# Attention scores of a latent-attention layer: the two heads of a pair in row tiles of 64, and a head's three rotary products in one pass of 96 rows

## The chip, the core and the metric

The kernel runs on one core of a Trainium2 chip, as one program. The metric is the device time of one execution in microseconds (us), lower being better. A core has TensorE (PE in the profile; PEld is its loading of weights), VectorE (DVE), ScalarE (ACT), GpSimd (POOL) and SyncE (SP, whose queue issues the DMAs here). TensorE multiplies a stationary operand of up to 128 rows by 128 columns, the "weights", with a moving operand of the same rows and up to 512 columns. The rows are the dimension that is summed over. The result stands in a PSUM bank of 128 partitions by 512 fp32 values.

## What is computed

One inference step of a two-layer backbone for 1024 latent ("sample") and 256 context ("prompt") tokens, 1280 in all, with a model width of 1024. The first layer is windowed attention beside a matrix-memory recurrence. The second, in which the change lies, is multi-head latent attention:

```python
def _mixer_c(h, w_in, q_norm, w_qb, kv_norm, w_kvb, w_out, ctx, pos):
    qa, kva, kr, z = jnp.split(h @ w_in, C_SPLITS, axis=-1)
    q = (_rmsnorm(qa, q_norm) @ w_qb).reshape(B, T, C_HEADS, C_NOPE + C_ROPE)      # 16 heads, 64 + 32
    q_nope, q_rope = q[..., :C_NOPE], q[..., C_NOPE:]
    ...                                            # rotary positions on q_rope and kr of the sample tokens
    kv = (keys_ckv @ w_kvb).reshape(B, Tk, C_HEADS, C_NOPE + C_VDIM)
    k_nope, v = kv[..., :C_NOPE], kv[..., C_NOPE:]
    k = jnp.concatenate([k_nope, jnp.broadcast_to(keys_kr, (B, Tk, C_HEADS, C_ROPE))], axis=-1)
    qf = jnp.concatenate([q_nope, q_rope], axis=-1)[:, :, :, None, :]
    attn = _blocked_attn(qf, k, v, None, (C_NOPE + C_ROPE) ** -0.5)                # softmax(q k) v
    out = (attn * jax.nn.silu(z)) @ w_out
```

A head's query and key have 64 values of their own ("nope") and 32 rotary ones; the rotary key is the same for all heads. Sample tokens read 1280 keys (1024 of their own and 256 of a cache), prompt tokens the 256 of the prompt.

## The kernel before

Every fp32 operand of a product is split into a high part, rounded to the type fp32r, and the rest as a low part. A product then is three: high by high, high by low, low by high.

The second layer's attention is the class `Mla`. It goes through eight pairs of heads (`pair`, p = 0 to 7). Keys of a pair (`keys`, in three chunks of 512), queries (`queries`, in chunks of 512, 512 and 256 tokens) and values are made from the latents by products on TensorE, and split by `split_sb`: a cast to the high part on ACT, a subtraction for the low part on DVE. `fill` lists at which step of a pair the keys, queries and values of the next are made.

For the scores each head has tiles of its own for its query and its key (`cQ`, `cK`; high and low), in which the 64 nope rows and the 32 rotary rows stand below each other: 96 rows for the first head of a pair. For the second the nope rows come out of the product in partitions 64 to 127, so its tiles have 128 rows: 32 rows of zeros in the query, the 32 rotary ones, and then the 64. `spread` splits the two heads' halves of a product into their tiles, 64 partitions at a time, and DMAs bring the rotary rows from DRAM.

`scores(p)` is a generator over blocks of 256 query tokens and, within a block, the two heads one after the other. `part` issues the three products of one head, 128 queries by 512 keys (`one`) or by 256 (`both`, twice into one bank). A bank `S` goes to a maximum on DVE (`cmx`) and an exponential on ACT (`cPa`, `cPb`, `cPc`), and `finish` scales by the sums on POOL. `uses` then transposes the probabilities on TensorE into a bank `T` (line 107), splits them (`cph` on ACT, `cpl` on DVE), and multiplies with the values into a bank `V`. `pair` advances both: a step of `scores`, a step of `uses` once more than six steps are ahead, and what `fill` has due. All products pass through the helper of line 103, so the profile's rows are told apart by their tiles. `set_psum(S=3, T=3, V=1, mm=1)` shares out PSUM's eight banks.

The order in which the engines get their instructions isn't that of the code: the framework's scheduler (`schedule_with_timeline_sim=True`) reorders the instructions of each engine by a simulated timeline. [...]

Of the kernel before, what the change touches and what calls it, by code (L numbers as in the profile page):

```python
# [22 lines left out]
T = TS + TP  # L23
# [1799 lines left out]
def split_sb(K, src, h, l, scale=None):  # L1823

    nc = K.nc
    if scale is None:
        nc.scalar.copy(h, src)
        nc.vector.tensor_sub(l, src, h.bitcast(F32))
    else:
        nc.scalar.mul(h, src, scale)  # L1830
        nc.vector.scalar_tensor_tensor(l, src, scale, h.bitcast(F32), ALU.mult, ALU.subtract)


def layer_c(K):
    nc, I, d = K.nc, K.I, K.dc
# [17 lines left out]
    ps = K.psT()  # L1853
# [21 lines left out]
    C = Mla(K, wp, cq, ckv)  # L1875
# [9 lines left out]
    for ci, (t0, N) in enumerate(CHUNKS):  # L1885
        for k in (0, 1, 2, 3, 4):
# [22 lines left out]
    cu.release()  # L1909
    ap = C.ap = left("catt")  # L1910
    C.add_queries(ap)
    C.add_values(ap, sets[1])
    for c in range(3):
        C.keys(0, c)
# [2 lines left out]
        for i in range(2):  # L1917
            C.values(0, c, i)
    C.add_set(ap)
    K.set_psum(S=3, T=3, V=1, mm=1)  # L1920
    for p in range(7):
        C.pair(p, C.fill(p))

# [39 lines left out]
class Mla:  # L1963

    SLOTS = ((3, 4, 5), (0, 1, 2), (3, 5, 0), (4, 6, 1), (0, 2, 4), (3, 5, 1), (4, 6, 3), (0, 2, 1))

    def __init__(self, K, wp, cq, ckv):
        self.K, self.wp, self.cq, self.ckv = K, wp, cq, ckv  # L1970
        self.w, self.KV, self.Q, self.queue = {}, [], [], []
        self.wv = {}
        self.use, self.ahead, self.tail = self.uses(), 0, None

    def add_set(self, pool):
        K, kr, n = self.K, self.K.dc["kr"], len(self.KV)
        keys = [[pool.tile([128, 1536], F32R, tag=f"cK{n}{par}{s}", name=f"cK{n}{par}{s}") for s in range(2)]
                for par in range(2)]
        for s in range(2):
            K.dma(keys[0][s][64:96, :], kr[s])  # L1980
            for o in (0, 32):
                K.dma(keys[1][s][o:o + 32, :], kr[s])
        self.KV.append(keys)

    def add_values(self, *pools):

# [5 lines left out]
        self.V = {(p, c): tiles[i] for p, row in enumerate(self.SLOTS) for c, i in enumerate(row)}  # L1992

    def add_queries(self, pool):
        K = self.K
        for c, (_, N) in enumerate(CHUNKS):
            t = [[pool.tile([128, N], F32R, tag=f"cQ{c}{par}{s}", name=f"cQ{c}{par}{s}") for s in range(2)]
                 for par in range(2)]
            for s in range(2):
                K.nc.gpsimd.tensor_scalar(t[1][s][0:32, :], K.small.rearrange("p a f -> p (a f)")[0:32, 0:N], 0.0, 1.0, ALU.mult, ALU.mult)  # L2000
            self.Q.append(t)

    def weights(self, p):
        K, wp, nc = self.K, self.wp, self.K.nc
# [29 lines left out]
    def spread(self, ps, dst, cols):  # L2034

        for par in range(2):
            r = slice(par * 64, par * 64 + 64)
            split_sb(self.K, ps[r], *[t[r, cols] for t in dst[par]])

    def keys(self, p, c):  # L2040
        ps = self.K.ps()
        self.products(ps, self.w[p][1], [t[c] for t in self.ckv], 2)
        self.spread(ps, self.KV[p % 2], slice(c * 512, (c + 1) * 512))

    def values(self, q, c, i):

# [10 lines left out]
    def queries(self, p, ci):  # L2057
        K, (t0, N) = self.K, CHUNKS[ci]
        ps = K.ps()
        self.products(ps[:, 0:N], self.w[p][0], [t[ci] for t in self.cq], 3)  # L2060
        self.spread(ps[:, 0:N], self.Q[ci], slice(0, N))
        for par, r in ((0, 64), (1, 32)):
            h = (2 * p + par) % 4 * 32
            for s in range(2):
                K.dma(self.Q[ci][par][s][r:r + 32, :], K.dc["qr"][s][p // 2][h:h + 32, t0:t0 + N])

    def fill(self, p):

        q = (p + 1) // 2
        f = [(0, partial(self.queries, p, 1)), (2, partial(self.queries, p, 2)), (4, partial(self.weights, p + 1))]  # L2070
        if p % 2:
            f += [(8, partial(self.weights_v, q))]
            f += [(14 + 4 * i, partial(self.values, q, i // 2, i % 2)) for i in range(4)]
        elif p:
            f += [(7 + i, partial(self.values, q, 2, i)) for i in range(2)]
# [12 lines left out]

    def finish(self):
        while self.use_step():  # L2090
# [9 lines left out]

    def scores(self, p):

        K, nc, ap, keys = self.K, self.K.nc, self.ap, self.KV[p % 2]
        for t0, par in ((t0, par) for t0 in range(0, T, 256) for par in range(2)):
            sample = t0 < TS
            ci = t0 // 512
            rows = slice(0, 128 if par else 96)
            Q, KK = [t[rows] for t in self.Q[ci][par]], [t[rows] for t in keys[par]]
            P = {}
            mx = K.t(ap, [128, 2, 3], F32, "cmx", 3)  # L2110
            den = K.t(ap, [128, 2, 3], F32, "cden", 3)

            def part(bank, bo, b, k0, n):
                q0 = t0 - CHUNKS[ci][0] + b * 128
                qs = slice(q0, q0 + 128)
                o = bank[:, bo:bo + n]
# [3 lines left out]
                return o  # L2120

            def finish(b):
                st = K.t(ap, [128, 8], F32, "cst", 4)
                nm, wt, dw, rd = st[:, 0:1], st[:, 1:4], st[:, 4:7], st[:, 7:8]
                if sample:
                    nc.vector.tensor_reduce(nm, mx[:, b, :], AX.X, ALU.min)
                    nc.scalar.activation(wt, mx[:, b, :], AF.Exp, bias=nm, scale=-1.0)
                    nc.gpsimd.tensor_mul(dw, den[:, b, :], wt)
                    nc.vector.reduce_sum(rd, dw, axis=AX.X)
                    nc.vector.reciprocal(rd, rd)  # L2130
                    for c in range(3):
                        pv = P[b, c]
                        nc.gpsimd.tensor_scalar(pv, pv, wt[:, c:c + 1], rd, ALU.mult, ALU.mult)  # L2133
                else:
                    nc.vector.reciprocal(rd, den[:, b, 0:1])
                    nc.gpsimd.tensor_scalar(P[b, 0], P[b, 0], rd, 1.0, ALU.mult, ALU.mult)

            def both(k0, c):
                S = K.psS()
                t = K.t(ap, [128, 512], F32, "cPc", 4)  # L2140
                for b in range(2):
                    part(S, b * 256, b, k0, 256)
                nc.vector.tensor_reduce(mx[:, :, c], S.rearrange("p (b k) -> p b k", b=2), AX.X, ALU.max, negate=True)
                for b in range(2):
                    P[b, c] = t[:, b * 256:(b + 1) * 256]
                    nc.scalar.activation(P[b, c], S[:, b * 256:(b + 1) * 256], AF.Exp,
                                         bias=mx[:, b, c:c + 1], accum_out=den[:, b, c:c + 1])

            def one(b, c):
                S = K.psS()  # L2150
                part(S, 0, b, c * 512, 512)
                nc.vector.tensor_reduce(mx[:, b, c:c + 1], S, AX.X, ALU.max, negate=True)  # L2152
                P[b, c] = K.t(ap, [128, 512], F32, "cP" + "ab"[c], 4)
                nc.scalar.activation(P[b, c], S, AF.Exp, bias=mx[:, b, c:c + 1],  # L2154
                                     accum_out=den[:, b, c:c + 1])

            if sample:
                one(0, 0)
                yield
                one(0, 1)  # L2160
                yield
                both(1024, 2)
                finish(0)
                yield
                one(1, 0)
                yield
                one(1, 1)
                finish(1)
            else:
                both(1280, 0)  # L2170
                finish(0)
                finish(1)
            self.queue.append((p, par, t0, P))
            yield

    def uses(self):
# [75 lines left out]
```

## Time and profile before

| | |
|---|---|
| runs shown | 2643.43, 2643.76, 2644.60 us; median 2643.76 |
| the profiled execution | 2644.84 us, its span 2643.0 us |
| granted TensorE clock | 0.995 of full speed |
| busy, share of the span | PE 97%, PEld 86%, DVE 67%, ACT 53%, POOL 44% |
| the second layer's attention | from 1875 to about 2540 us |

The span is the time from the first to the last instruction. In the profile's rows a group is named by line, engine, operation and "out<-in" tiles with the sizes (rows*columns of the weights, then partitions x elements of the output or of the moving operand); behind "x" stands the count, then the busy time in us and the mean duration in ns, then the engine's idle time ahead of the group and what ended it. [...] In rows of single instructions the first number is the start in us and the second the duration; "x3" are three of a kind in a row.

### The profile page before, as it was taken

The page shows a single profiled execution, that of the slowest core. Times are in us where ns is not written, and L with a number is a line of the kernel's source. Part 1 is how long each engine was busy: PE and PEld are TensorE (multiplying, and loading weights), DVE is VectorE, ACT ScalarE, POOL GpSimd, SP SyncE. Part 2 cuts the span into 40 slices and gives each one's busy share as a digit, 9 for nine tenths or more (in the row PEclk, how much of TensorE's full clock was granted, in tenths as well). Part 3 has the DMA queues.
Part 4 walks back from the last instruction along what each step waited for, and adds up shares of the span by engine and source line. Part 5 has one row for each costly group of instructions (what it writes and reads, how often), then busy time and mean ns, then how long its engine had stood idle before and what let it go on. Part 6 is the DMA issues. An engine that isn't in the chain of part 4 may idle for free.

```text
span 2643.0 us, 48201 instructions
## 1 busy us (share of the span) xinstructions
PE 2572.9 (97%) x16209; PEld 2262.3 (86%) x16209; DVE 1777.3 (67%) x4040; ACT 1406.5 (53%) x3598; POOL 1167.1 (44%) x1533
## 2 busy tenths in 40 slices
PE   7989999999999999989999999999899999999998
PEld 6878899898998888868888877987799999999887
DVE  6883565655746666388777545335788888888853
ACT  5222443543533433287666533322788888888842
POOL 4342333423434434275545453223455545555642
PEclk9989999999999999999999999999999999999999
DMA  7554556556657655463433463333311101101333
GB/s 247 181 157 157 161 178 198 175 171 195 199 169 225 213 164 185 140 204 111 136 102 111 130 197 130 121 95 114 104 30 30 44 29 40 35 19 30 122 104 128
DMA packets 344586, 348.79 MB, mean 132 GB/s; under 512 B 29610, under 2 KB 291415, under 8 KB 344083
## 3 DMA queue, kind: packets, MB, share of 16 engines
q1 hardware_dynamic: 344338, 345.71, 42.1%
q8 instruction: 129, 2.11, 0.3%
q14 instruction: 119, 0.97, 0.1%
HBM read 235.09 MB, written 110.51 MB: 131 GB/s over the span
## 4 chain that ended last, share of the span: by engine, by line
PE 81%; DVE 6%; DMA 3%; ACT 3%; issue 3%; POOL 2%; SPq 1%; POOLq 0%; DVEq 0%; ACTq 0%
PE mm L103 34%; PE S L103 27%; PE V L103 8%; PE T L107 6%; PE D L103 3%; PE mm L107 2%; SPq L138 1%; PE T L103 1%; DVE macc L321 1%; DVE att_nm L1109 0%; DVE xT L536 0%; ACT att_p L1114 0%; POOL wl L354 0%; DMA o_x<-y 0%; DMA w<-in_w_out_ab 0%
## 5 line engine op out<-in xcount | busy, mean ns | idle before, releaser
L354 POOL TENSOR_TENSOR wl<-wf,wh 128x256 fp32r<-128x256 f32 (+2 forms) x288 | 250.7, 896 | 448.6 <-ACT wh L353 378.6
L103 PE MATMUL mm<-hTh,wh 128*128 128x512 f32 (+1 forms) x912 | 328.6, 360 | 1.6 <-DVE scr L620 0.9
L103 PE MATMUL mm<-hTl,wh 128*128 128x512 f32 (+1 forms) x912 | 325.5, 357 | 0.0
L103 PE MATMUL mm<-hTh,wl 128*128 128x512 f32 (+1 forms) x912 | 325.4, 357 | 0.0
L103 PE MATMUL S<-cK,cQ 96*128 96x512 f32 (+3 forms) x1248 | 298.3, 364 | 3.3 <-ACT cPb L2154 1.0
L2202 DVE TENSOR_TENSOR cpl<-T,cph 128x512 fp32r<-128x512 f32 x336 | 228.5, 685 | 38.0 <-ACT cph L2201 34.5
L103 PEld LDWEIGHTS S<-cK,cQ 96*128 96x128 f32 (+1 forms) x1248 | 192.8, 189 | 25.9 <-ACT cPb L2154 2.9
L2201 ACT CAST cph<-T 128x512 fp32r<-128x512 f32 x336 | 192.3, 589 | 26.6 <-PE T L107 13.4
L103 PEld LDWEIGHTS mm<-hTh,wl 128*128 128x128 f32 x912 | 172.0, 189 | 26.4
L103 PEld LDWEIGHTS mm<-hTh,wh 128*128 128x128 f32 x912 | 171.9, 188 | 25.7 <-DVE bmod L306 1.7
L103 PEld LDWEIGHTS mm<-hTl,wh 128*128 128x128 f32 x912 | 171.9, 188 | 22.9
L2152 DVE TENSOR_REDUCE cmx<-S 128x1 f32<-128x512 f32 x256 | 172.7, 681 | 16.4 <-PE S L103 15.2
L103 PE MATMUL V<-cph,cV 128*128 128x256 f32 x672 | 177.0, 290 | 1.0 <-DVE co L2217 1.0
L103 PE MATMUL V<-cpl,cV 128*128 128x256 f32 x672 | 171.9, 285 | 1.3 <-DVE cpl L2202 1.3
L103 PE MATMUL S<-w,o_ah 128*128 128x512 f32 x492 | 152.1, 395 | 3.0 <-ACT w L819 1.9
L103 PE MATMUL mm<-w,o_ah 128*128 128x512 f32 x468 | 151.4, 402 | 0.0
L2133 POOL TENSOR_SCALAR cPa<-cPa,cst 128x512 f32<-128x512 f32 x128 | 99.3, 776 | 118.0 <-DVE cst L2130 87.5
L1123 POOL TENSOR_SCALAR att_p<-att_p,att_den 128x640 f32<-128x640 f32 (+1 forms) x128 | 97.5, 774 | 103.4 <-DVE att_den L1120 41.0
L1134 ACT CAST att_ph<-mm 128x512 fp32r<-128x512 f32 x168 | 98.5, 586 | 81.5 <-PE mm L107 80.0
L353 ACT CAST wh<-wf 128x256 fp32r<-128x256 f32 (+2 forms) x288 | 102.0, 409 | 70.1 <-DMA wf<-in_w_in_ab 30.5
L1135 DVE TENSOR_TENSOR att_pl<-mm,att_ph 128x512 fp32r<-128x512 f32 x168 | 115.7, 689 | 32.1 <-ACT att_ph L1134 27.3
L103 PE MATMUL mm<-wh,hTh 128*128 128x256 f32 x480 | 135.8, 283 | 0.0
(432 smaller groups left out, 7823.5 us busy)
## 6 DMA issues: line engine op xcount, KB each, us to landing
wf<-in_w_in_ab SPq DMA_DIRECT2D x120, 256.0 KB
in<-in SPq DMA_DIRECT2D x40, 514.0 KB
in<-in SPq DMA_DIRECT2D x32, 386.0 KB
mw<-in_w_mod SPq DMA_DIRECT2D x48, 256.0 KB
in<-scr SPq DMA_DIRECT2D x40, 258.0 KB
o_x<-y SPq DMA_DIRECT2D x20, 512.0 KB
wm<-in_w_mod SPq DMA_DIRECT2D x16, 512.0 KB
in<-cx SPq DMA_DIRECT2D x32, 256.0 KB
```

The costliest lines, as they stand in the source:

```text
L103: return self.nc.tensor.matmul(out, lhsT, rhs, start=start, stop=stop)
L107: self.nc.tensor.transpose(out, in_, self.ident[:p, :p])
L138: self.nc.sync.dma_start(f(out), f(in_))
L353: K.nc.scalar.copy(wh, wf[:, k])
L354: K.nc.gpsimd.tensor_sub(wl, wf[:, k], wh.bitcast(F32))
L1123: nc.gpsimd.tensor_scalar(pv, pv, den[:, i:i + 1], 1.0, ALU.mult, ALU.mult)
L1134: K.nc.scalar.copy(ph, self.T)
L1135: K.nc.vector.tensor_sub(pl, self.T, ph.bitcast(F32))
L2133: nc.gpsimd.tensor_scalar(pv, pv, wt[:, c:c + 1], rd, ALU.mult, ALU.mult)
L2152: nc.vector.tensor_reduce(mx[:, b, c:c + 1], S, AX.X, ALU.max, negate=True)
L2201: nc.scalar.copy(ph, T_)
L2202: nc.vector.tensor_sub(pl, T_, ph.bitcast(F32))
```

## The change

The nope rows and the rotary rows get products of their own.

- Nope: one tile of 128 rows holds both heads' 64 rows, for keys and for queries. `part` works on both heads at once, with a bank each, and alternates between them: the three products of the first head have rows 0 to 63, those of the second rows 64 to 127.
- Rotary: the three products of a head (high by high, high by low, low by high) are put below each other in 3 x 32 = 96 rows: `cQr` holds the query's high, high and low parts, `cKr` the key's high, low and high. One product of 96 rows adds all three to the bank. `cKr` is loaded once for all pairs.
- `spread` and the zero rows fall away: a product of keys or queries is split over 128 partitions at once. The loads of rotary query rows become six per chunk instead of four; those of the rotary keys three instead of twelve.
- `scores` yields once for both heads and `pair` counts two steps for it, starting `uses` at more than ten steps ahead. Statistics and probabilities have more buffers. PSUM has four banks `S` and two `T`, instead of three and three.

```diff
-    K.set_psum(S=3, T=3, V=1, mm=1)
+    K.set_psum(S=4, T=2, V=1, mm=1)
...
     def add_set(self, pool):
-        keys = [[pool.tile([128, 1536], F32R, tag=f"cK{n}{par}{s}", name=f"cK{n}{par}{s}") for s in range(2)]
-                for par in range(2)]
-        for s in range(2):
-            K.dma(keys[0][s][64:96, :], kr[s])
-            for o in (0, 32):
-                K.dma(keys[1][s][o:o + 32, :], kr[s])
-        self.KV.append(keys)
+        n = len(self.KV)
+        self.KV.append([pool.tile([128, 1536], F32R, tag=f"cK{n}{s}", name=f"cK{n}{s}") for s in range(2)])
+
+    def add_rotary(self, pool):
+        K = self.K
+        self.kr = pool.tile([96, 1536], F32R, tag="cKr", name="cKr")
+        for i, s in enumerate((0, 1, 0)):
+            K.dma(self.kr[i * 32:i * 32 + 32, :], K.dc["kr"][s])
...
     def keys(self, p, c):
-        self.spread(ps, self.KV[p % 2], slice(c * 512, (c + 1) * 512))
+        split_sb(self.K, ps, *[t[:, c * 512:(c + 1) * 512] for t in self.KV[p % 2]])
...
     def queries(self, p, ci):
-        self.spread(ps[:, 0:N], self.Q[ci], slice(0, N))
-        for par, r in ((0, 64), (1, 32)):
+        split_sb(K, ps[:, 0:N], *self.Q[ci])
+        for par in range(2):
             h = (2 * p + par) % 4 * 32
-            for s in range(2):
-                K.dma(self.Q[ci][par][s][r:r + 32, :], K.dc["qr"][s][p // 2][h:h + 32, t0:t0 + N])
+            for i, s in enumerate((0, 0, 1)):
+                K.dma(self.QR[ci][par][i * 32:i * 32 + 32, :], K.dc["qr"][s][p // 2][h:h + 32, t0:t0 + N])
...
-            self.ahead += 1
-            if self.ahead > 6 and self.use_step():
-                next(self.use)
-            while fill and fill[0][0] <= n:
-                fill.pop(0)[1]()
-            n += 1
+            self.ahead += 2
+            for _ in range(2):
+                if self.ahead > 10 and self.use_step():
+                    next(self.use)
+                while fill and fill[0][0] <= n:
+                    fill.pop(0)[1]()
+                n += 1
...
-        for t0, par in ((t0, par) for t0 in range(0, T, 256) for par in range(2)):
+        for t0 in range(0, T, 256):
...
-                K.mm(o, Q[0][:, qs], KK[0][:, k0:k0 + n], True, False)
-                K.mm(o, Q[0][:, qs], KK[1][:, k0:k0 + n], False, False)
-                K.mm(o, Q[1][:, qs], KK[0][:, k0:k0 + n], False, True)
+                for i, (q, k) in enumerate(((qh, kh), (qh, kl), (ql, kh))):
+                    for par in range(2):
+                        r = slice(par * 64, par * 64 + 64)
+                        K.mm(banks[par][:, bo:bo + n], q[r, qs], k[r, ks], i == 0, False)
+                for par in range(2):
+                    K.mm(banks[par][:, bo:bo + n], QR[par][:, qs], self.kr[:, ks], False, True)
```

What becomes of the order on TensorE, as the two programs are built. The first place is the start of the third block of sample tokens (queries 512 to 767) of the first pair. Before, TensorE's queue holds this for the first head, where each number behind `S` is a bank of scores (128 queries by 512 keys):

```order
L103 MATMUL S_23370<-cK_22274,cQ_22673 128x512
L103 MATMUL S_23370<-cK_22275,cQ_22673 128x512
L103 MATMUL S_23370<-cK_22274,cQ_22674 128x512
L103 MATMUL V_23116<-cph_23217,cV_22689 128x256
L103 MATMUL S_23390<-cK_22274,cQ_22673 128x512
L103 MATMUL S_23390<-cK_22275,cQ_22673 128x512
L103 MATMUL S_23390<-cK_22274,cQ_22674 128x512
```

In the changed program TensorE's queue has this for the same block; `S_23308` and `S_23358` are banks of the first head, in rows 0 to 63, `S_23309` is one of the second, in rows 64 to 127, and `cKr,cQr` is the product of 96 rows:

```order
L103 MATMUL S_23308<-cK_22274,cQ_22663 128x512
L103 MATMUL S_23308<-cK_22275,cQ_22663 128x512
L103 MATMUL S_23308<-cK_22274,cQ_22664 128x512
L103 MATMUL S_23308<-cKr,cQr_22665 128x512
L103 MATMUL S_23309<-cK_22274,cQ_22663 128x512
L103 MATMUL S_23309<-cK_22275,cQ_22663 128x512
L103 MATMUL S_23309<-cK_22274,cQ_22664 128x512
L103 MATMUL S_23309<-cKr,cQr_22666 128x512
L103 MATMUL S_23358<-cK_22274,cQ_22663 128x512
L103 MATMUL S_23358<-cK_22275,cQ_22663 128x512
L103 MATMUL S_23358<-cK_22274,cQ_22664 128x512
L103 MATMUL S_23358<-cKr,cQr_22665 128x512
```

The code issues the products of the two banks in turns; the scheduler has moved them apart, so that one head's three and its rotary product come before the other head's.

The second place is TensorE's queue in the same block, for queries 640 to 767. Before, the first head's products of that bank stand between products for the next queries (`mm`) and transposes:

```order
L103 MATMUL mm_24004<-cq_22254,wql_22969 128x512
L103 MATMUL S_23446<-cK_22274,cQ_22673 128x512
L103 MATMUL S_23446<-cK_22275,cQ_22673 128x512
L103 MATMUL S_23446<-cK_22274,cQ_22674 128x512
L107 MATMUL T_23355<-small,cPb_23114 128x128
```

In the changed program the two heads' banks for these queries stand in TensorE's queue like this:

```order
L103 MATMUL S_23482<-cK_22274,cQ_22663 128x512
L103 MATMUL S_23483<-cK_22274,cQ_22663 128x512
L103 MATMUL S_23482<-cK_22275,cQ_22663 128x512
L103 MATMUL S_23483<-cK_22275,cQ_22663 128x512
L103 MATMUL S_23482<-cK_22274,cQ_22664 128x512
L103 MATMUL S_23483<-cK_22274,cQ_22664 128x512
L103 MATMUL S_23482<-cKr,cQr_22665 128x512
L103 MATMUL S_23483<-cKr,cQr_22666 128x512
```

Here the turns are kept; of 128 places with products of 512 columns, three are left in this way.

More of the change, by code (lines that the diff above doesn't have):

```diff
@@ L1911, in layer_c @@
     C.add_queries(ap)
+    C.add_rotary(ap)
     C.add_values(ap, sets[1])
@@ L1970, in __init__ @@
         self.K, self.wp, self.cq, self.ckv = K, wp, cq, ckv
-        self.w, self.KV, self.Q, self.queue = {}, [], [], []
+        self.w, self.KV, self.Q, self.QR, self.queue = {}, [], [], [], []
         self.wv = {}
@@ L1994, in add_queries @@
     def add_queries(self, pool):
-        K = self.K
         for c, (_, N) in enumerate(CHUNKS):
-            t = [[pool.tile([128, N], F32R, tag=f"cQ{c}{par}{s}", name=f"cQ{c}{par}{s}") for s in range(2)]
-                 for par in range(2)]
-            for s in range(2):
-                K.nc.gpsimd.tensor_scalar(t[1][s][0:32, :], K.small.rearrange("p a f -> p (a f)")[0:32, 0:N], 0.0, 1.0, ALU.mult, ALU.mult)
-            self.Q.append(t)
+            self.Q.append([pool.tile([128, N], F32R, tag=f"cQ{c}{s}", name=f"cQ{c}{s}") for s in range(2)])
+            self.QR.append([pool.tile([96, N], F32R, tag=f"cQr{c}{par}", name=f"cQr{c}{par}") for par in range(2)])
     def weights(self, p):
@@ L2032, in products @@
                 self.K.mm(out, st[a][:, k, :], mv[b][:, k, :], k + i == 0, k == kt - 1 and i == 2)
[L2034 to L2038, printed above, removed]
     def keys(self, p, c):
@@ L2074, in fill @@
         elif p:
-            f += [(7 + i, partial(self.values, q, 2, i)) for i in range(2)]
+            f += [(12 + i, partial(self.values, q, 2, i)) for i in range(2)]
         f += [(12 + 6 * c, partial(self.keys, p + 1, c)) for c in range(3)]
@@ L2101, in scores, with part, finish @@
     def scores(self, p):
-        K, nc, ap, keys = self.K, self.K.nc, self.ap, self.KV[p % 2]
-        for t0, par in ((t0, par) for t0 in range(0, T, 256) for par in range(2)):
+        K, nc, ap, (kh, kl) = self.K, self.K.nc, self.ap, self.KV[p % 2]
+        for t0 in range(0, T, 256):
             sample = t0 < TS
             ci = t0 // 512
[L2107 to L2113, printed above, removed]
-                q0 = t0 - CHUNKS[ci][0] + b * 128
-                qs = slice(q0, q0 + 128)
-                o = bank[:, bo:bo + n]
-                K.mm(o, Q[0][:, qs], KK[0][:, k0:k0 + n], True, False)
-                K.mm(o, Q[0][:, qs], KK[1][:, k0:k0 + n], False, False)
-                K.mm(o, Q[1][:, qs], KK[0][:, k0:k0 + n], False, True)
-                return o
-            def finish(b):
-                st = K.t(ap, [128, 8], F32, "cst", 4)
+            (qh, ql), QR = self.Q[ci], self.QR[ci]
+            P = [{}, {}]
+            mx = [K.t(ap, [128, 2, 3], F32, "cmx", 6) for _ in range(2)]
+            den = [K.t(ap, [128, 2, 3], F32, "cden", 6) for _ in range(2)]
+            def part(banks, bo, b, k0, n):
+                q0 = t0 - CHUNKS[ci][0] + b * 128
+                qs, ks = slice(q0, q0 + 128), slice(k0, k0 + n)
+                for i, (q, k) in enumerate(((qh, kh), (qh, kl), (ql, kh))):
[4 more added lines that the diff above has]
+                    K.mm(banks[par][:, bo:bo + n], QR[par][:, qs], self.kr[:, ks], False, True)
+            def finish(par, b):
+                st = K.t(ap, [128, 8], F32, "cst", 8)
@@ L2124, in finish @@
                 nm, wt, dw, rd = st[:, 0:1], st[:, 1:4], st[:, 4:7], st[:, 7:8]
                 if sample:
-                    nc.vector.tensor_reduce(nm, mx[:, b, :], AX.X, ALU.min)
-                    nc.scalar.activation(wt, mx[:, b, :], AF.Exp, bias=nm, scale=-1.0)
-                    nc.gpsimd.tensor_mul(dw, den[:, b, :], wt)
+                    nc.vector.tensor_reduce(nm, mx[par][:, b, :], AX.X, ALU.min)
+                    nc.scalar.activation(wt, mx[par][:, b, :], AF.Exp, bias=nm, scale=-1.0)
@@ L2129, in finish @@
+                    nc.gpsimd.tensor_mul(dw, den[par][:, b, :], wt)
                     nc.vector.reduce_sum(rd, dw, axis=AX.X)
@@ L2131, in finish @@
                     for c in range(3):
-                        pv = P[b, c]
+                        pv = P[par][b, c]
                         nc.gpsimd.tensor_scalar(pv, pv, wt[:, c:c + 1], rd, ALU.mult, ALU.mult)
                 else:
-                    nc.vector.reciprocal(rd, den[:, b, 0:1])
-                    nc.gpsimd.tensor_scalar(P[b, 0], P[b, 0], rd, 1.0, ALU.mult, ALU.mult)
+                    nc.vector.reciprocal(rd, den[par][:, b, 0:1])
+                    nc.gpsimd.tensor_scalar(P[par][b, 0], P[par][b, 0], rd, 1.0, ALU.mult, ALU.mult)
@@ L2138, in both @@
             def both(k0, c):
-                S = K.psS()
-                t = K.t(ap, [128, 512], F32, "cPc", 4)
+                banks = [K.psS() for _ in range(2)]
                 for b in range(2):
[L2142 to L2147, printed above, removed]
@@ L2149, in one @@
-            def one(b, c):
[L2150 to L2155, printed above, removed]
+                    part(banks, b * 256, b, k0, 256)
+                for par, S in enumerate(banks):
+                    t = K.t(ap, [128, 512], F32, "cPc", 4)
+                    nc.vector.tensor_reduce(mx[par][:, :, c], S.rearrange("p (b k) -> p b k", b=2), AX.X, ALU.max,
+                                            negate=True)
+                    for b in range(2):
+                        P[par][b, c] = t[:, b * 256:(b + 1) * 256]
+                        nc.scalar.activation(P[par][b, c], S[:, b * 256:(b + 1) * 256], AF.Exp,
+                                             bias=mx[par][:, b, c:c + 1], accum_out=den[par][:, b, c:c + 1])
@@ new lines, in one @@
+            def one(b, c):
+                banks = [K.psS() for _ in range(2)]
+                part(banks, 0, b, c * 512, 512)
+                for par, S in enumerate(banks):
+                    nc.vector.tensor_reduce(mx[par][:, b, c:c + 1], S, AX.X, ALU.max, negate=True)
+                    P[par][b, c] = K.t(ap, [128, 512], F32, "cP" + "ab"[c], 8)
+                    nc.scalar.activation(P[par][b, c], S, AF.Exp, bias=mx[par][:, b, c:c + 1],
+                                         accum_out=den[par][:, b, c:c + 1])
@@ L2162, in scores @@
                 both(1024, 2)
-                finish(0)
+                for par in range(2):
+                    finish(par, 0)
                 yield
@@ L2167, in scores @@
                 one(1, 1)
-                finish(1)
+                for par in range(2):
+                    finish(par, 1)
             else:
                 both(1280, 0)
-                finish(0)
-                finish(1)
-            self.queue.append((p, par, t0, P))
+                for par in range(2):
+                    for b in range(2):
+                        finish(par, b)
+            for par in range(2):
+                self.queue.append((p, par, t0, P[par]))
             yield
```

2 lines of the change are left out of this document (removed).

## Prediction

> **What bounds the kernel now.** I read the page's busy times and its chain first, then the busy times of the stage that the change touches (the attention of the second layer, 1875 to 2540 us), then its groups by shape, and last single TensorE instructions by start time.
>
> ```profile
> PE 2572.9 (97%) x16209; PEld 2262.3 (86%) x16209; DVE 1777.3 (67%) x4040; ACT 1406.5 (53%) x3598; POOL 1167.1 (44%) x1533
> PE 81%; DVE 6%; DMA 3%; ACT 3%; issue 3%; POOL 2%; SPq 1%; POOLq 0%; DVEq 0%; ACTq 0%
> core 0: us, PE busy (x) PEld busy (x) DVE busy (x) ACT busy (x) POOL busy (x), PEclk, DMA share, GB/s
> 1800.00:1875.00 75.00, 64.83 (x367) 54.39 (x365) 45.83 (x81) 29.34 (x62) 30.36 (x27) 0.95 0.47 146
> 1875.00:2540.00 665.00, 657.40 (x4512) 596.64 (x4513) 567.74 (x1300) 558.57 (x1531) 363.26 (x610) 1.00 0.14 44
> PE T L107 <- DVE cpl L2202: 1.8, 3, 0.8
> ```
>
> In the stage TensorE (PE) is busy for 657.4 of 665 us at full clock, and its longest wait in all is 1.8 us, on VectorE. DVE (568) and ACT (559) have some 100 us to spare. So a microsecond of PE work put in or taken out moves the end by about one; work saved on the other engines moves nothing. What a PE instruction costs is the distance between starts, since the printed durations overlap:
>
> ```profile
> 2142.69 0.86 PE L103 MATMUL S<-cK,cQ 128*128 128x512 f32 x3
> 2143.38 0.28 PE L103 MATMUL V<-cpl,cV 128*128 128x256 f32 x1
> 2143.73 0.60 PE L107 MATMUL T<-small,cPa 128*128 128x128 f32 x4
> 2150.80 0.88 PE L103 MATMUL S<-cK,cQ 96*128 96x256 f32 x6
> 2151.51 0.28 PE L103 MATMUL V<-cpl,cV 128*128 128x256 f32 x1
> L103 PE MATMUL S<-cK,cQ 96*128 96x512 f32 x384 | 114.3, 410 | 1.1 <-PE mm L103 1.0
> L103 PE MATMUL S<-cK,cQ 128*128 128x512 f32 x384 | 112.8, 407 | 1.1 <-ACT cPa L2154 0.6 <-ACT cPc L2146 0.5
> L103 PE MATMUL S<-cK,cQ 96*128 96x256 f32 x240 | 38.6, 293 | 0.0
> L103 PE MATMUL S<-cK,cQ 128*128 128x256 f32 x240 | 38.3, 291 | 1.1 <-ACT cPb L2154 1.0
> ```
>
> Three score products of 512 columns take 2142.69 to 2143.38, or 0.23 us each; six of 256 columns take 2150.80 to 2151.51, or 0.118 each. 96 rows cost what 128 cost. All score products: 768 x 0.232 + 480 x 0.1175 = 178 + 56 = 235 us.
>
> **The extra products.** Per head and bank there were three products; now there are three of 64 rows and one of 96. By themselves that is a third more: 256 x 0.232 + 160 x 0.1175 = 59 + 19 = **+78 us**. It is paid back only where a product in rows 0 to 63 runs at the same time as one in rows 64 to 127. If every one found its partner, half of 235 would go (117 us), and the net would be -39.
>
> **How many find it.** The scheduler does not keep the order in which the code writes them. Counted over the new PE order, of 1248 products of 64 rows only 21 (512 columns) and 18 (256) neighbours are in different row tiles; the usual run is three products of one head, its rotary product, then something else. Each product pairs once, which leaves about 12 and 11 pairs: 12 x 0.232 + 11 x 0.1175 = **-4 us**. No row of this trace shows two row tiles side by side; the bounds are 0 and -4.
>
> **The changes of row tile.** The new order enters the tile of 64 rows 424 times in this layer and leaves it 424 times, nearly always to the rotary product next. Before, it did so never there. What such a change costs shows where the first layer puts a transpose of few rows between wide products:
>
> ```profile
> 246.76 0.39 PE L103 MATMUL mm<-hTh,wl 128*128 128x512 f32 x1
> 246.99 0.40 PE L103 MATMUL mm<-hTh,wh 128*128 128x512 f32 x1
> 247.32 0.24 PE L107 MATMUL T<-small,modrow 32*128 32x32 f32 x1
> 247.49 0.50 PE L103 MATMUL mm<-hTl,wh 128*128 128x512 f32 x1
> 247.83 0.40 PE L103 MATMUL mm<-hTh,wl 128*128 128x512 f32 x1
> 247.31 0.13 PEld L107 LDWEIGHTS T<-small,modrow 32*128 32x128 f32 x1 [0.36 <-PE mm L103]
> 247.49 0.19 PEld L103 LDWEIGHTS mm<-hTl,wh 128*128 128x128 f32 x1
> 247.60 0.19 PEld L103 LDWEIGHTS mm<-hTh,wl 128*128 128x128 f32 x1
> 154.24 0.40 PE L103 MATMUL S<-hTh,wl 128*128 128x512 f32 x1
> 154.57 0.81 PE L107 MATMUL T<-small,rst 36*128 36x36 f32 x10
> 155.22 0.79 PE L107 MATMUL T<-small,gM 36*128 36x36 f32 x10
> 155.94 0.49 PE L103 MATMUL S<-hTh,wh 128*128 128x512 f32 x1
> 156.27 0.40 PE L103 MATMUL S<-hTl,wh 128*128 128x512 f32 x1
> ```
>
> Wide products start 0.23 apart (246.76, 246.99). Before the small one it is 0.33: 0.10 of standstill, and its weight load begins only at 247.31, where loads otherwise begin with the product before. Back again, the load starts with its own product (247.49) and the next start comes after 0.34: 0.11 of load that nothing covers, the 0.11 between the two loads. The rows at 154 to 156 (36 rows) give the same: 0.33 in, 0.33 out. The ten transposes there take 0.065 each, load and all; the one at 247.32 takes 0.17, so leaving costs 0.10 too. A change of tile thus costs 0.095 of standstill and 0.105 of bare load, 0.20 us, and in and out 0.40: 424 x 0.40 = 170 us. Of the entries 136 stand behind transposes, which start 0.11 apart ((0.60 - 0.27) / 3) though 128 columns stream in 0.23 / 4 = 0.058; some 0.05 of the standstill falls into that: -7. **+162 us.**
>
> The rows are of fp32 transposes; the new switches are between products, so the price is bounded by nothing from below and by the full 0.40 from above. I take 0.40, since both halves of the load and standstill appear at wide products of the same type, going in and coming out. [...]
>
> **What costs nothing.** Keys and queries are split once over 128 rows instead of twice over 64:
>
> ```profile
> L1827 ACT CAST cK<-mm 64x512 fp32r<-64x512 f32 x42 | 24.4, 580 | 3.6 <-DVE cK L1828 2.3 <-PE mm L103 0.7
> L1828 DVE TENSOR_TENSOR cK<-mm,cK 64x512 fp32r<-64x512 f32 x42 | 28.8, 685 | 2.9 <-ACT cK L1827 2.0
> L2201 ACT CAST cph<-T 128x512 fp32r<-128x512 f32 x330 | 188.9, 589 | 25.5 <-PE T L107 12.5 <-PE V L103 10.8
> L2202 DVE TENSOR_TENSOR cpl<-T,cph 128x512 fp32r<-128x512 f32 x330 | 224.4, 685 | 36.8 <-ACT cph L2201 33.5
> ```
>
> A cast takes 580 ns at 64 rows and 589 at 128, so half of them goes: 12 us of ACT and 14 of DVE on the keys, about as much on the queries. Both lie beside a full PE: 0. The rotary loads on SP's queue grow from 96 to 144, and the twelve of the keys become three; they are asked for at steps 0, 2 and 33 of a pair's 42 and read from steps 20, 40 and 42, at least nine steps of 665 / 8 / 42 = 2 us ahead, and no wait of PE on a DMA stands in the list whose first row is above: 0. Banks for transposed probabilities go from three to two. One is held for 0.44 + 0.59 + 0.69 = 1.7 us plus waits, so two pass one every 0.9 us, and 336 are needed in some 900 us, one per 2.7: 0. Without that cover, 0.1 us at each would be +34. Going the other way, PE's 7.6 us of idle time could be taken up.
>
> **Sum**, against the profiled execution's own 2644.84 us (span 2643.0): 2644.8 + 78 - 4 + 162 = 2881; less 1.1, since the median of the runs shown is 2643.76: **2880 us**. Its own range is 2840 to 2925: the idle time and price roundings (0.36 instead of 0.40 is -17) below, the T banks above.
>
> **Rivals.**
> - *Weights of the same tile are not loaded ahead* (12%). In runs of three, the second and third product would wait for a bare load: 1248 - 424 - 39 = 785 x 0.105 = +82: 2962. Against it: the ten transposes in one row tile take 0.065 each, no more than their load. [...]
> - *Only one half of the price* (12%), standstill or load: 424 x 0.20 - 4 = 81: 2644 + 74 + 81 = 2799.
> - *The change of tile is free between products* (7%): 2644 + 74 = 2718. For it: all rows of a price are next to transposes. Against: the load held back at 247.49 is that of a plain product.
> - *The other side: the heads do overlap* (3%): TensorE would have to run a head's rows 64 to 127 beside the other's across the rotary product between them, with free changes. With a share f of paired products the time changes by 78 - 117 f; it turns at f = 2/3, and at 1 gives 2605. The order gives f = 0.035.
>
> **Chances and range.** The forecast has 66%. From the half price up to the bare loads, 2795 to 2965, the range leaves out the free change, the overlap and some of the edges. A lower clock, as the 0.95 of the stage ahead, would add 5% of 900 us, 45, and lies inside. A measurement of this kernel can tell 0.2% (5 us) from no change: slower 96%, faster 3%, the same 1%.
>
> **What would show it.** In the profile after: 1248 score products of 64 rows and 416 of 96; the stage from 665 to about 900 us; starts 0.33 apart on entering and on the rotary product after leaving; loads beginning with their own product there; PE's clock still 1.00; ACT and DVE casts halved with no effect. I am wrong if 64-row products start next to the rotary one at 0.23, if they start in pairs a few ns apart in many places, or if PE waits for T banks by tens of us.

## The result, and the profile after

| | before | changed |
|---|---|---|
| median of four runs, us | 2644.18 | 2931.47 |
| lowest to highest | 2643.43 to 2645.12 | 2922.82 to 2941.99 |
| profiled execution, us (span) | 2644.84 (2643.0) | 2932.68 (2930.9) |
| granted TensorE clock | 0.995 | 0.975 |

The ratio is 1.109 (95% interval 1.105 to 1.113): 287 us slower, where 236 were forecast. The time is inside the range of 2795 to 2965, but 6 us above 2840 to 2925, the range of the sum by itself.

From the page of the changed kernel, the busy times and the chain by line:

```profile
PE 2865.9 (98%) x16625; PEld 2369.2 (81%) x16625; DVE 1773.4 (61%) x3992; ACT 1394.1 (48%) x3550; POOL 1162.3 (40%) x1527
PE S L103 35%; PE mm L103 31%; PE V L103 8%; PE T L107 6%; PE D L103 3%; PE mm L107 2%; PE T L103 1%; DVE att_nm L1109 0%; DVE cpl L2204 0%; SPq L138 0%; ACT att_p L1114 0%; ACT cph L2203 0%; POOL wl L354 0%; POOL w L820 0%; DMA w<-in_w_out_ab 0%
```

The busy times of the engines in the stage (us, PE, PEld, DVE, ACT, POOL, then PE's clock, DMA share, GB/s):

```profile
1875.00:2820.00 945.00, 938.24 (x4849) 693.93 (x4850) 557.95 (x1240) 539.70 (x1468) 360.31 (x607) 0.94 0.11 33
```

The longest of PE's own waits there (in total, times, longest):

```profile
PE V L103 <- DVE cpl L2204: 3.9, 15, 0.4
```

PE fills the stage as before, and waits for others by a few us. (`PE S` in the chain isn't the score products alone: banks of the first layer bear the name `S` too.) One number was not expected: the clock in the stage is 0.94, where it was 1.00. The groups of score products by shape:

```profile
L103 PE MATMUL S<-cK,cQ 64*128 64x512 f32 x768 | 257.8, 447 | 1.0 <-DVE cV L1828 0.9
L103 PE MATMUL S<-cKr,cQr 96*128 96x512 f32 x256 | 132.0, 519 | 0.0
L103 PE MATMUL S<-cK,cQ 64*128 64x256 f32 x480 | 100.9, 321 | 0.8 <-ACT cPa L2152 0.8
L103 PE MATMUL S<-cKr,cQr 96*128 96x256 f32 x160 | 61.6, 392 | 0.0
```

Single instructions on PE in order of time, at full clock (start, duration):

```profile
2202.62 0.28 PE L103 MATMUL V<-cph,cV 128*128 128x256 f32 x1
2202.84 0.96 PE L103 MATMUL S<-cK,cQ 64*128 64x512 f32 x3
2203.72 0.50 PE L103 MATMUL S<-cKr,cQr 96*128 96x512 f32 x1
2204.07 0.28 PE L103 MATMUL V<-cpl,cV 128*128 128x256 f32 x1
...
2205.34 0.60 PE L107 MATMUL T<-small,cPa 128*128 128x128 f32 x4
2205.86 0.96 PE L103 MATMUL S<-cK,cQ 64*128 64x512 f32 x3
```

There are 1248 products of 64 rows and 416 of 96, as counted ahead. From the product at 2202.62 to the first of the tile of 64 rows pass 0.22 us, where 0.118 is usual: 0.10 of standstill. The three products take 0.88, and 3 x 0.232 = 0.70: the rest, 0.18, is the bare load at the first and the standstill after the last, 0.105 and 0.095 in the forecast. The rotary product takes 0.35, 0.12 over: the bare load of the way back. That makes 0.10 + 0.18 + 0.12 = 0.40 for a round trip, one entry and one exit. So a tile change costs what the transposes of the first layer showed, and the second and third product of a tile have no bare load. Behind four transposes (2205.34) the next start comes after 0.52, of which the first three transposes take 0.33: 0.19 for the last, 0.08 more than its usual 0.11.

The clock shows where a pair begins. Three products and the rotary one of 256 keys, four times in a row, and what follows, again in order of time:

```profile
2106.03 0.61 PE L103 MATMUL S<-cK,cQ 64*128 64x256 f32 x3
2106.57 0.39 PE L103 MATMUL S<-cKr,cQr 96*128 96x256 f32 x1
2106.89 0.62 PE L103 MATMUL S<-cK,cQ 64*128 64x256 f32 x3
2107.44 0.38 PE L103 MATMUL S<-cKr,cQr 96*128 96x256 f32 x1
...
2109.67 1.64 PE L103 MATMUL S<-cK,cQ 64*128 64x512 f32 x3
2111.24 0.79 PE L103 MATMUL S<-cKr,cQr 96*128 96x512 f32 x1
```

The weight loads of the second such round begin with their own products, as the forecast had it:

```profile
2106.89 0.41 PEld L103 LDWEIGHTS S<-cK,cQ 64*128 64x128 f32 x3
2107.43 0.19 PEld L103 LDWEIGHTS S<-cKr,cQr 96*128 96x128 f32 x1
```

The busy times and the clock (the third number from the end) of the 3.4 us of these products and of the 3.4 us after:

```profile
2105.70:2109.10 3.40, 3.40 (x16) 2.29 (x16) 2.47 (x5) 2.29 (x7) 0.00 (x0) 1.00 0.00 0
2109.10:2112.50 3.40, 3.40 (x11) 2.18 (x9) 1.81 (x4) 0.00 (x0) 0.73 (x1) 0.51 0.26 77
```

From 2109.1 the clock is at half: three products of 512 now take 1.57 (2109.67 to 2111.24) instead of 0.88. Each of the six middle pairs has one such stretch of 10.2 us, at its start; the first and the last pair have several. Over the stage, 0.06 of 945 us is 57 us of clock.

### The profile page after: what moved, and what is told of

The parts are those of the page before. It is cut to its first block, busy times and chain, and to the rows that moved or that the text cites. A ratio compares the mean times of both kernels' runs of the same rounds, so it can differ in the third digit from the quotient of the medians.

```text
span 2930.9 us, 48602 instructions
## 1 busy us (share of the span) xinstructions
PE 2865.9 (98%) x16625; PEld 2369.2 (81%) x16625; DVE 1773.4 (61%) x3992; ACT 1394.1 (48%) x3550; POOL 1162.3 (40%) x1527
## 4 chain that ended last, share of the span: by engine, by line
PE 84%; DVE 3%; issue 2%; ACT 2%; DMA 2%; POOL 1%; SPq 0%; DVEq 0%; POOLq 0%; ACTq 0%
PE S L103 35%; PE mm L103 31%; PE V L103 8%; PE T L107 6%; PE D L103 3%; PE mm L107 2%; PE T L103 1%; DVE att_nm L1109 0%; DVE cpl L2204 0%; SPq L138 0%; ACT att_p L1114 0%; ACT cph L2203 0%; POOL wl L354 0%; POOL w L820 0%; DMA w<-in_w_out_ab 0%
## 5 line engine op out<-in xcount | busy, mean ns | idle before, releaser
L103 PE MATMUL S<-cK,cQ 64*128 64x512 f32 (+1 forms) x1248 | 358.7, 399 | 1.7 <-DVE cV L1828 0.9
L103 PEld LDWEIGHTS S<-cK,cQ 64*128 64x128 f32 x1248 | 194.6, 193 | 95.0 <-issue 34.5
L103 PE MATMUL V<-cph,cV 128*128 128x256 f32 x672 | 201.5, 315 | 1.2 <-DVE co L2219 1.1
L103 PE MATMUL S<-cKr,cQr 96*128 96x512 f32 (+1 forms) x416 | 193.6, 470 | 0.0
L103 PE MATMUL V<-cpl,cV 128*128 128x256 f32 x672 | 186.9, 300 | 3.9 <-DVE cpl L2204 3.9
L103 PEld LDWEIGHTS S<-cKr,cQr 96*128 96x128 f32 x416 | 79.5, 193 | 116.7 <-issue 97.2
L2123 POOL TENSOR_TENSOR cst<-cden,cst 128x3 f32<-128x3 f32 x128 | 24.8, 199 | 339.5 <-ACT cPc L2143 181.0
L103 PEld LDWEIGHTS V<-cpl,cV 128*128 128x128 f32 x672 | 135.0, 201 | 14.2 <-DVE cpl L2204 7.1
L103 PEld LDWEIGHTS V<-cph,cV 128*128 128x128 f32 x672 | 135.1, 201 | 7.0 <-DVE co L2219 1.3
```

What stands on the lines that cost most here:

```text
L103: return self.nc.tensor.matmul(out, lhsT, rhs, start=start, stop=stop)
L2123: nc.gpsimd.tensor_mul(dw, den[par][:, b, :], wt)
```

## The experiments

Differences are against the median of the kernel before as it ran beside each of them: 2649.32 for the full rows without tile change, the two banks, the small products of 64 rows and the rotary product in the head's row tile; 2647.25 for the small products of all rows and the full rows in the 256-key banks; 2644.99 for the other four.

**Full rows, no tile change.** In `part` of the changed kernel:

```diff
-                        r = slice(par * 64, par * 64 + 64)
+                        r = slice(0, 128)
```

> The changed kernel, with its nope products over all 128 rows of the shared tiles (so each head gets the sum of both heads; the separation of the heads is left out). Same count of products and the same banks, but no change of row tile anywhere in the layer. Theory (third more products 78, changes of tile 162, half clock 50): only the 78 us stay, 2722 us, and the clock is 1.00 in the stage as before. Rival, the time lies in the banks (two for transposes, four for scores), the order or the waits of the new loop: it stays near 2900. Rival, the half clock comes from the new order alone and not from the changes of tile: 2770.

Measured: 2731.80, +82 (ratio 1.032, 1.030 to 1.033), and the busy times of the stage, at a clock of 1.00:

```profile
1875.00:2600.00 725.00, 716.30 (x4756) 645.39 (x4755) 533.45 (x1223) 526.79 (x1451) 353.60 (x598) 1.00 0.14 40
```

The third more products are worth what was forecast, 78. The new loop, its banks and its order cost at most 4.

**Two banks as one tile.** So that both heads can start at once:

```diff
-    K.set_psum(S=4, T=2, V=1, mm=1)
+    K.set_psum(S=2, T=2, V=1, mm=1)
+    K.two = lambda: K.t(K.psum["S"], [128, 1024], F32, "S")
+    K.psS = lambda: K.two()[:, 0:512]
...
-                banks = [K.psS() for _ in range(2)]
+                banks = (lambda t: [t[:, 0:512], t[:, 512:1024]])(K.two())
...
```

The last change stands twice, in `both` and in `one`.

> The changed kernel, with the two banks of a step taken as one tile of two banks, so that both heads can start at once; the order then has the two heads' products in turns at nearly every place, and enters the tile of 64 rows 246 times instead of 424. Theory (products in rows 0 to 63 and 64 to 127 run at the same time, and a change of tile costs 0.20 us in either direction): 78 of more products, -114 by overlap, +94 by changes: 2702 us, plus half clock of at most 30. Rival, products in two row tiles don't overlap on this chip: 2816 plus the half clock. Rival, changes of tile cost nothing: 2608.

Measured: 2741.68, +92 (ratio 1.036, 1.034 to 1.037). PE's instructions in order of time:

```profile
2205.42 0.96 PE L103 MATMUL S<-cK,cQ 64*128 64x512 f32 x6
2206.31 0.73 PE L103 MATMUL S<-cKr,cQr 96*128 96x512 f32 x2
2206.98 0.62 PE L103 MATMUL S<-cK,cQ 64*128 64x256 f32 x6
2207.53 0.50 PE L103 MATMUL S<-cKr,cQr 96*128 96x256 f32 x2
```

The busy times of its stage:

```profile
1875.00:2620.00 745.00, 712.88 (x4800) 559.62 (x4801) 543.76 (x1234) 531.77 (x1457) 361.09 (x606) 1.00 0.14 41
```

Six products of 512 keys take 0.89, as long as three in the changed kernel; the two heads overlap fully. That is the gain of the forecast's other side, but the changes of tile remain, and PE now idles for 32 us of the stage (745.00 less 712.88; 7.6 before). Of the +92, 58 are the expected sum; of the 34 above it, 24 are the added idle time.

**Small products ahead of full ones.** In `part` of the kernel before, first with 64 rows, then with all rows as a control:

```diff
                 o = bank[:, bo:bo + n]
+                K.mm(o[:, 0:32], Q[0][0:64, qs], KK[0][0:64, k0:k0 + 32], True, True)
```

> The kernel before, with one small product of 64 rows and 32 columns ahead of each head's three score products (its result is overwritten; nothing is left out): 416 changes into the tile of 64 rows and 416 out, with all other products full. Theory, a change of tile costs 0.095 of standstill and 0.105 of bare load: 416 x 0.42, less 7 behind transposes, 2825 us, and if the standstill is what lowers the clock, some tens more, with half-clock stretches at full-row products. Rival, only products of 64 rows in long runs bring the clock down: 2825 with the clock at 1.00. Rival, changes of tile are nearly free: 2660.

```diff
                 o = bank[:, bo:bo + n]
+                K.mm(o[:, 0:32], Q[0][:, qs], KK[0][:, k0:k0 + 32], True, True)
```

> The kernel before with one small product of 128 rows and 32 columns ahead of each head's three (overwritten; nothing left out): the same 416 small products as with 64 rows (153 over before), without a change of tile. Theory: a small product costs the 0.105 of a weight load, 416 x 0.105 = 44, less some 10 of waits taken up: 25 to 45 over before, so that some 115 of the 153 are the changes of tile. Rival, the small products themselves (their issue, their bank) cost most of it: 100 or more.

Measured: with 64 rows 2802.25, +153 (ratio 1.058, 1.057 to 1.060), where 176 to 181 were expected; with all rows 2685.53, +38 (1.014, 1.012 to 1.017). The expectation's terms for 64 rows don't add up to its 2825: 2644 + 175 - 7 = 2812, or +168. The small product as such costs 38 / 416 = 0.09 us, about the 0.105 of a bare weight load; the other 115 of the 153 come with the changes of tile. By the price of the forecast, 0.40 and 0.01 for the small product's 32 columns, 416 x 0.41 = 170. PE idles for 2 us of this stage instead of 7.6, which is 6 of the 17 us of difference; the rest stays open. The clock stays at 1.00 with 64 rows (busy times of the stage):

```profile
1875.00:2680.00 805.00, 802.96 (x4839) 666.61 (x4839) 576.03 (x1284) 565.29 (x1515) 356.75 (x600) 1.00 0.12 35
```

**The rotary product in the head's row tile.** In the changed kernel (the loads of `cKr` and `cQr` follow):

```diff
-                    K.mm(banks[par][:, bo:bo + n], QR[par][:, qs], self.kr[:, ks], False, True)
+                    r = slice(par * 64, par * 64 + 64)
+                    K.mm(banks[par][:, bo:bo + n], QR[par][r, qs], self.kr[r, ks], False, True)
```

> The changed kernel, with the rotary product in the head's own row tile of 64 (high by high and high by low; the low-by-high third of the rotary part is left out), so that no change of tile stands between a head's nope and rotary products: 287 entries instead of 424, with 19 us of overlap instead of 4. Theory: 2644 + 78 - 19 + 105 = 2808 us, plus a half clock of 0 to 30. Rival, the time lies in the 64-row products as such, not in the changes: it stays within 20 us of 2931. Rival, changes free: 2703.

Measured: 2797.73, +148 (ratio 1.057, 1.055 to 1.058), where 164 were expected; clock 1.00 in the stage. This is 133 us less than the changed kernel's +281 when it ran again (below): 137 round trips fewer are 55, the overlap 15, the half clock that is gone some 44 (below), and 19 stay unaccounted for. The 64-row products as such are not what costs.

**All products in tiles of 64, in pairs.** The two-bank form, with the rotary part as two products of 64 rows, `[qh; qh]` and `[ql; 0]` against `[kh; kl]` (the two-bank part of the edit, as above, and the loads of `cKr` and `cQr` aren't shown):

```diff
-                for par in range(2):
-                    K.mm(banks[par][:, bo:bo + n], QR[par][:, qs], self.kr[:, ks], False, True)
+                for i in range(2):
+                    for par in range(2):
+                        r = slice(par * 64, par * 64 + 64)
+                        K.mm(banks[par][:, bo:bo + n], QR[i][r, qs], self.kr[r, ks], False, i == 1)
```

> The two-bank form, with the rotary products in the heads' row tiles of 64 as well (two products of 64 rows instead of one of 96; nothing left out). Entries into the tile of 64 rows: 240, hardly fewer than the 246 of the two-bank form. Theory: five products for each pair of heads in turns, -32 against before with the overlap, +91 to 98 for the changes, and some 25 of waits for banks as in the two-bank form: 85 to 90 us over before. Rival, the waits of the two-bank form come from its rotary products standing alone: 60 over before.

Measured: 2748.54, +104 (ratio 1.039, 1.037 to 1.041): above the 85 to 90. PE's longest wait in the stage is now one of transposes, for the split that frees their bank:

```profile
PE T L107 <- DVE cpl L2211: 15.9, 12, 1.8
```

The busy times of its stage:

```profile
1875.00:2640.00 765.00, 728.72 (x5275) 573.82 (x5274) 548.64 (x1244) 536.39 (x1468) 361.99 (x609) 0.99 0.14 43
```

PE idles for 36 us of it, 16 of them in this wait. Where the products overlap, the two banks `T` seem to limit, as far as this wait shows; with three of them it wasn't tried.

**The changed kernel again.**

> The changed kernel again, beside the others of this call. Theory: 285 us over before, with stretches of half clock at the start of each pair. Rival, the half clock was an accident of one chip: 237 over before, clock 1.00 in the stage.

Measured: 2926.28, +281 (ratio 1.107, 1.104 to 1.109), clock 0.95 in the stage: the half clock is the kernel's, since it came on another chip too.

**Full rows and tile changes.** In `part`, on top of the full rows:

```diff
+                        if i == 0:
+                            K.mm(banks[par][:, bo:bo + 32], q[0:64, qs], k[0:64, k0:k0 + 32], True, True)
```

> The changed kernel with its nope products over all 128 rows (each head gets the sum of both, the separation is left out) and a small product of 64 rows and 32 columns ahead of each head's three, overwritten by them: 414 entries into the tile of 64 rows, as many large products as the changed kernel, but with full rows. If the half clock comes from the standstill at changes of tile: 285 over before, with the same half-clock stretches. If it comes from products that fill half the rows: 82 (as measured with full rows alone) + 414 x 0.41 = 252, less some 10 of waits taken up, about 240 over before, clock 1.00.

Measured: 2888.75, +244 (ratio 1.092, 1.091 to 1.094). The busy times of the stage:

```profile
1875.00:2700.00 825.00, 821.57 (x4847) 683.95 (x4847) 505.40 (x1148) 495.15 (x1364) 314.60 (x554) 1.00 0.09 26
```

This is the forecast's sum, products and tile changes, at full clock; 244 - 82 = 162 for 414 round trips is 0.39 each, with some 0.01 of it for the small product's own columns. Standstill in this dose, 414 round trips, left the clock at 1.00 where the products have full rows.

**Full rows in the 256-key banks alone.** The changed kernel with

```diff
-                        r = slice(par * 64, par * 64 + 64)
+                        r = slice(par * 64, par * 64 + 64) if n == 512 else slice(0, 128)
+                        if n == 256 and i == 0:
+                            K.mm(banks[par][:, bo:bo + 32], q[0:64, qs], k[0:64, k0:k0 + 32], True, True)
```

> The changed kernel, in which only the banks made of two halves of 256 keys have their nope products over all 128 rows (the separation of the heads is left out there), with a small product of 64 rows and 32 columns ahead of each three, overwritten, so that the changes of tile stay (416 entries); the products of 512 keys are those of the changed kernel. If the half clock is brought on by the stretches of 256-key products at the start of each pair, whose products fill half the rows between many changes of tile: the stretches are gone, clock 1.00, about 240 over before. Rival, the 512-key products bring it on as well: stays near 280.

Measured: 2884.02, +237 (ratio 1.090, 1.087 to 1.093), 44 less than the changed kernel's +281, at nearly as many tile changes. The busy times of the stage:

```profile
1875.00:2700.00 825.00, 821.55 (x4641) 625.57 (x4640) 514.52 (x1157) 496.99 (x1370) 322.00 (x563) 1.00 0.10 28
```

So the 256-key stretches bring the half clock here: with full rows in them the stage is at 1.00, where it was at 0.95.

**Twice the tile changes, full rows.** The kernel before, with small products of 64, 128 and 64 rows ahead of each three:

```diff
+                K.mm(o[:, 0:32], Q[0][0:64, qs], KK[0][0:64, k0:k0 + 32], True, True)
+                K.mm(o[:, 0:32], Q[0][:, qs], KK[0][:, k0:k0 + 32], True, True)
+                K.mm(o[:, 0:32], Q[0][0:64, qs], KK[0][0:64, k0:k0 + 32], True, True)
```

> The kernel before with three small products of 32 columns ahead of each head's three (64 rows, all rows, 64 rows; all overwritten): 832 entries into the tile of 64 rows and as many exits, with all large products full. Theory, 0.41 us in and out, with nothing more to take up: 153 (as measured for 416) + 416 x 0.41 = 324 over before, clock 1.00. If the standstill lowers the clock, this has twice as much of it as the changed kernel: long half-clock stretches and 380 or more.

Measured: 3032.68, +388 (ratio 1.146, 1.144 to 1.149), 64 above the 324; at a clock of 0.94, the 0.06 of a stage of some 1050 us are 63. The busy times of the stage:

```profile
1875.00:2700.00 825.00, 824.63 (x4540) 686.53 (x4539) 470.05 (x1027) 455.11 (x1211) 272.55 (x475) 0.94 0.08 22
```

This goes against a reading by rows alone: with 832 small entries instead of 416 the clock falls at full rows too, from 1.00 to 0.94. One quantity fits all of them, the share of rows and time that is filled, an estimate from the products' starts in these traces and the rows of each, of 128. For a round of three 256-key products and what stands between, with 0.118 us for a product: changed kernel, (3 x 0.118 x 64/128 + 0.118 x 96/128) / (0.47 + 0.40) = 30%, half clock; this kernel, 3 x 0.118 / (0.354 + 0.82) = 30%, half clock; small products once, 0.354 / (0.354 + 0.41) = 46%, full; full rows with changes, (0.354 + 0.089) / (0.47 + 0.41) = 50%, full. The 512-key rounds of the changed kernel, (3 x 0.232 / 2 + 0.232 x 0.75) / (0.93 + 0.40) = 39%, ran at full clock where they stood alone (1.00 from 2202.00 to 2204.50).

The traces allow a wider count. In the stage the clock changes only at steps of 3.41 us (in the changed kernel from 1.00 to 0.50 at 2109.10 and back at 2119.34, after three of them). For each step at full clock in the attention stage of the twelve traces (before, changed and ten experiments) the fill can be estimated: columns x 0.453 ns (0.232 us / 512) x rows / 128, summed over the products in it. The clock fell after 51 steps (13 of them in the changed kernel), and each of these was filled to 41% at most. Another 55 steps as empty as that kept the clock; none of the 2653 fuller ones lost it. Without the weight of the rows the two kinds don't part: steps in which products ran up to 74% of the time were followed by a fall, and 1145 with less kept the clock. So the estimated fill of rows and time is what parts them here, with a border that is blurred between some 30 and 41%; what exactly the chip counts stays open, and a kernel that sets the fill in small steps wasn't tried.

## Why the prediction was right, and by what it fell short

- *PE bounds the stage, and its sum is the end.* Right: 938 of 945 us busy and waits of a few us. That the work saved on ACT and DVE moves nothing fits, but no run tried it by itself.
- *Extra products, +78.* Right: +82 by themselves.
- *The scheduler parts the heads, -4.* Right in what it rests on: in the trace 25 products start within 12 ns of one in the other row tile, where some 23 were counted on, and the 424 entries are all there. Kept together, the heads overlap (six products in 0.89), so the rival that they can't is out, and it is the order that lost the 117.
- *Changes of tile, +162.* Right: 244 - 82 = 162 by the run with full rows. That it is the very number is chance: it is for 414 round trips, with some 6 us for the columns of the small products. The rivals go: bare loads in the same tile (three products take 0.88, so that their second and third load are covered), half the price (0.39 measured), none.
- *The 7 us off behind transposes.* Wrong at the one place shown: 0.08 stands still there too, where I took 0.095 less 0.05. For 136 entries that would be some 5 us.
- *Banks for transposes, 0.* Right here: PE's transposes waited 0.8 us in the stage for the split that frees their bank. In the last of the paired forms it was 15.9.
- *The clock.* This is the step that failed. I named "PE's clock still 1.00" as a sign, and put a lower clock among the edges of the range without a mechanism. It was 0.94 in the stage, 57 us of clock, and the 44 us between the changed kernel and the one with full rows in its 256-key banks are most of the 51 that the forecast fell short: 82 - 4 + 162 + 44 = 284, of the 287 measured. The 45 us that I named for a lower clock came from the row of 0.95 between 1800 and 1875. That was no row for this stage: PE had 65 of 75 us there, and idle time was all it could point at. I read PE as filled because it had an instruction in it all the time; standing still for a tile change and half the rows empty don't show in that.
- *The range.* That it held is in part luck: the sum's own range ended at 2925, and 2965 was set by a rival, the bare loads, that the runs refute.

## What to carry to other kernels

By the prices of these runs row tiles would pay only where both tiles run at the same time (six products in 0.89, where one head's three took 0.88) with few changes of tile between, and no run here reached that: a round trip costs 0.37 (153 / 416) to 0.40 us (from 2202.62), and pairing saves at most one product, 0.232 us, per pair of banks. With the full gain of 39 us, fewer than 39 / 0.40 = 98 round trips would have had to do, an estimate, and there were 424, or 246 in the form in which the heads did overlap. Before counting on products side by side, read the order that the scheduler makes of them: what it parted by banks was paid in full here, 0.88 for each head's three. And count not only PE's busy time but how much of the rows that time fills, since the clock went with it here: 0.94 in a stage with PE busy for 938 of 945 us.

## What the runs showed of the hardware that was not expected

- In the changed kernel the clock fell to half in stretches of 3.4 to 10.2 us while PE had an instruction at every moment (3.40 of 3.40 us from 2105.70), where products filled about 30% of rows and time by the estimate above; after steps filled to more than 41% it fell in none of the stages. The window from 2109.10 stands at 0.51 and those from 2112.50 to 2119.30 at 0.50, all at 3.40 of 3.40 us too, so that "busy" as the profile counts it doesn't decide.
- Two products of 64 rows in different row tiles took as long as one of them: 0.89 for six of 512 columns with the heads in turns, 0.88 for three of one head.
